# Seven block products in place of eight for five of 22 k-pairs of each down column pair

## The chip, the cores and the metric

The kernel runs on one core of one Trainium2 chip. The metric is device time in microseconds (us) of one execution; the kernel before has a median of 1750.02 us.

## The reference, cut to what matters

One decoder layer over 256 tokens of width 2048, in float32: an FFN, a mixing part (gated linear attention and dilated attention behind one input projection), an output projection, a second FFN. The change touches the two FFNs, above all their last product, `@ w_down`, with 5632 rows and 2048 columns.

```python
def swiglu(x, w_gate, w_up, w_down):
    return (jax.nn.silu(x @ w_gate) * (x @ w_up)) @ w_down
...
        x = x + FFN_RESIDUAL_WEIGHT * swiglu(rms_norm(x, ffn1_norm[l]), ffn1_w_gate[l], ffn1_w_up[l], ffn1_w_down[l])
        h = rms_norm(x, mix_norm[l])
        z = h @ w_in[l]
...
        x = x + FFN_RESIDUAL_WEIGHT * swiglu(rms_norm(x, ffn2_norm[l]), ffn2_w_gate[l], ffn2_w_up[l], ffn2_w_down[l])
    return x
```

## The kernel before

**Products.** Each float32 operand is split into a high and a low part (fp32r), and a product is three matmuls: high by high, high by low, low by high (`products`, lines 264, 266, 268). Activations stand transposed, 128 features by 256 tokens per k-tile: `hh` and `hl` (16 k-tiles) feed the gate, up and mixing products, `uh` and `ul` (44 k-tiles) the down products. The 256 tokens are two row blocks (t = 0, 1). A column pair is two blocks of 512 output columns and uses four PSUM banks. One k-tile of a column pair is a unit of 2 row blocks x 2 column blocks x 3 = 12 matmuls of 512 columns.

**Weights.** One DMA on SyncE's queue brings the weights of a k-pair (two k-tiles by 1024 columns, 1 MB) into one of three `raw` buffers. `prepare` splits a k-tile: ScalarE writes the high part `wh` (line 104), VectorE the low part `wl` (line 105), each 128 x 1024, into one of four buffers. `weights` keeps two prepared tiles ahead.

**Sevens.** In blocks 1 to 7 of the 11 gate-and-up blocks, k-pairs 2 and 5 (`GROUPS`) are multiplied as 2 x 2 blocks with seven products in place of eight (`seven_products`, lines 288 to 290): 21 matmuls in place of 24. These need sums of weights (`seven`, lines 228 and 236: a first and a last `raw` tile and two sums, so 3.5 splits in place of 2), sums of activations (`seven_forms`, lines 310 to 315, once per FFN, kept in `fh` and `fl`), four more banks for the products that go to more than one output, and five instructions that fold those banks into sums for the evacuation (lines 349 to 353). The four gate banks and the four of the sevens change places from block to block.

**Down.** `column_pair` runs the 44 units of each of the two column pairs in the order of k. At its end `evac` adds half of the result to the residual stream `xs` (line 454). In the first FFN each finished 128 x 512 block of `xs` is then normalised and transposed for the mixing part: for columns 0 to 1023 by `norm_moved` (VectorE transposes 32 x 32 squares, line 119; 16 small DMAs on GpSimd's queue, line 124, move them into `hh[8..15]`; `finish`, line 144 and `split`, writes `hh` and `hl` 0 to 7), for the rest by `norm_block` (TensorE, line 100).

**Order of the work.** Work beside the products stands in the list `later`; `column_pair` and `seven_pair` take from it at a steady rate, two steps a unit, over `span` steps. That is the order of the program's text. The order in which each engine issues is fixed when the program is built (`schedule_with_timeline_sim=True`), by a planner that has its own costs for every instruction and takes what it expects to be ready. Small 128 x 512 scratch tiles (`t512`: `sg`, `u`, `us`, `hf`) share four buffers.

Of the kernel before, what the change touches and what calls it, by code (L numbers as in the profile page):

```python
# [30 lines left out]
GROUPS = (2, 5)  # L31
SEVEN = range(1, 8)
TAIL = FT - 4 * SEVEN[-1] - 4
# [3 lines left out]
C_QG, C_KG, C_VG, C_GL, C_RG, C_QA, C_KA, C_VA = 0, 512, 1024, 2048, 2064, 3088, 4112, 5136  # L37


def layer_kernel(tc, x, xT, gains, gla_gate_up, gla_gate_bias, gla_out_norm, att_q_norm, att_k_norm,  # L40
# [6 lines left out]
    with ExitStack() as es:  # L47
# [27 lines left out]
        xs = cst.tile([P, NT, D], F32, name="xs")  # L75
        hh = cst.tile([P, KT, S], F32R, name="hh")
        hl = cst.tile([P, KT, S], F32R, name="hl")
# [7 lines left out]
        junk = cst.tile([P, 512], F32, name="junk")  # L85

# [46 lines left out]
        def norm_moved(t, c, gi):  # L133
# [13 lines left out]
            later.extend([lambda: None] * 4 + [finish])  # L147
# [13 lines left out]
        def ff_jobs(w):  # L161

            n = KT // 2
            for i in range(w.shape[0]):
                if i // n in SEVEN and i % n in GROUPS:
                    yield from ((w, i, part) for part in ("plain", "last", "sums", "more"))
                else:
                    yield from ((w, i, k) for k in range(2))

        jobs = [*ff_jobs(w_ff1)] + [(w_dn1, i, k) for i in range(w_dn1.shape[0]) for k in range(2)]  # L170
# [3 lines left out]
        jobs += [*ff_jobs(w_ff2)] + [(w_dn2, i, k) for i in range(w_dn2.shape[0]) for k in range(2)]  # L174
# [9 lines left out]
        def prepare():  # L184
# [15 lines left out]
            if k in ("last", "sums", "more"):  # L200
                return seven(k)
# [7 lines left out]
            if k == "plain":  # L209
                return seven(k)  # L210
# [9 lines left out]
        room = {}  # L220

        def seven(part):

            raw = raws[0].bitcast(F32)
            if part == "plain":
# [44 lines left out]
        later = []  # L270

# [4 lines left out]
        def seven_products(cs, ms, kp, first, last):  # L276
# [6 lines left out]
            fh, fl = room["fh"], room["fl"]  # L283
            a11, a12, a22 = [(hh[:, 2 * kp + k, tok[t]], hl[:, 2 * kp + k, tok[t]]) for t, k in ((0, 0), (0, 1), (1, 1))]
            s1, s3, s2, sa = [(fh[kp][:, i, :], fl[kp][:, i, :]) for i in range(4)]
# [17 lines left out]
        def seven_forms(kp):  # L303

            raw = room["rest"][0], room["rest"][1]
            full = raw[0].rearrange("p (k t q) -> p k t q", k=2, t=NT)
            sums = raw[1].rearrange("p (i q) -> p i q", i=4)
            ks = slice(2 * kp, 2 * kp + 2)
            nc.vector.tensor_add(raw[0].rearrange("p (k s) -> p k s", k=2), hh[:, ks, :].bitcast(F32), hl[:, ks, :].bitcast(F32))
            a11, a12, a21, a22 = full[:, 0, 0, :], full[:, 1, 0, :], full[:, 0, 1, :], full[:, 1, 1, :]  # L310
# [6 lines left out]
        def seven_pair(b, evac):  # L317

            cs = four_banks(b % 2)
            ms = None  # L320
            folds = []
            order[0] = 4 * (1 - b % 2)
            units = []
            for kp in range(KT // 2):
                units += [kp] if kp in GROUPS else [(2 * kp,), (2 * kp + 1,)]
            total = done = 0
            steps = 2 * (len(units) - len(GROUPS))
            step = 0
            for n, unit in enumerate(units):
                if isinstance(unit, tuple):  # L330
                    ws = [weights()]
                    for t in range(NT):
                        step += 1
                        total = max(total, done + len(later))
                        go = min(max(-(-total * step // steps) - done, 0), len(later))
# [4 lines left out]
                        products([cs[2 * t], cs[2 * t + 1]], t, [hacts[unit[0]]], ws, n == 0, n == len(units) - 1)  # L340
                    continue
                if ms is None:
                    ms = four_banks(1 - b % 2)
                last = unit == GROUPS[-1]
                seven_products(cs, ms, unit, unit == GROUPS[0], last)
                if last:
                    nat = [m.rearrange("p (a b) -> p b a", b=2) for m in ms]
                    p1, u, u2, u3 = [halves(a) for a in room["rest"]]
                    folds = [lambda: nc.scalar.activation(p1, nat[0], AF.Copy),
                             lambda: nc.vector.tensor_add(u, p1, nat[2]),  # L350
                             lambda: nc.vector.tensor_add(u2, u, nat[3]),
                             lambda: nc.vector.tensor_add(u, u, nat[1]),
                             lambda: nc.vector.tensor_add(u3, u2, nat[1])]
            for t in range(NT):
                rest = ((u, p1), (u3, u2))[t]
                evac(t, [c.rearrange("p (a b) -> p b a", b=2) for c in cs[2 * t:2 * t + 2]], rest)
# [516 lines left out]
```

## Time and profile before

| what | value |
|---|---|
| median of 3 runs | 1750.02 us (1748.29 to 1750.72) |
| profiled execution, its own time | 1748.53 us |
| its span, first to last instruction | 1746.8 us |
| granted TensorE clock over the span | 1.000 of full speed |
| weights read, queue of SyncE | 350.25 MB, 55.9% of 16 DMA engines |

The span is what the instructions cover; the profiled execution's own time is 1.7 us more. All terms below are read from this one execution. PE is TensorE's matmul, PEld its weight load, DVE VectorE, ACT ScalarE, POOL GpSimd, SP SyncE.

### The profile page before, as it was taken

How to read it: one execution, taken by the hardware profiler on the slowest of the kernel's cores; microseconds unless marked ns; L12 is line 12 of the kernel's file. 1: busy time of each engine (PE TensorE's matmuls, PEld its weight loads, DVE VectorE, ACT ScalarE, POOL GpSimd, SP SyncE). 2: the span in 40 equal slices, each digit the busy share in tenths (PEclk: the TensorE clock that was granted, in tenths of full speed). 3: DMA queues.
4: the chain of work that ended last, by engine and by line, in shares of the span. 5: the costliest groups of instructions: out<-in, count | busy, mean ns of one | idle time of the engine just before them, and what ended most of it. 6: DMA issues, size and time to landing. Idle time of an engine off the chain costs nothing.

```text
span 1746.8 us, 21964 instructions
## 1 busy us (share of the span) xinstructions
PE 1736.6 (99%) x8160; PEld 1515.7 (87%) x8160; DVE 1179.1 (68%) x1329; ACT 885.2 (51%) x1088; POOL 438.4 (25%) x870
## 2 busy tenths in 40 slices
PE   9999999999999999999999999999999999999999
PEld 7888888888888888888888888888888888888887
DVE  7888888855544656566655657788888955554544
ACT  7555555544444445565654545555555544444442
POOL 0333344443300421011000034333333444310000
PEclk9999999999999999999999999999999999999999
DMA  8666565766655666556444464666665666665653
GB/s 341 225 220 217 207 228 207 253 213 218 216 201 209 211 222 212 194 193 215 156 166 169 146 220 165 229 218 235 231 222 215 223 215 215 222 214 201 225 208 121
DMA packets 80843, 367.59 MB, mean 210 GB/s; under 512 B 19248, under 2 KB 36656, under 8 KB 38496
## 3 DMA queue, kind: packets, MB, share of 16 engines
q1 hardware_dynamic: 50864, 350.25, 55.9%
q0 software_dynamic: 29152, 14.87, 3.3%
q8 instruction: 64, 1.05, 0.2%
q10 hardware_dynamic: 720, 1.07, 0.2%
q14 instruction: 43, 0.35, 0.1%
HBM read 350.38 MB, written 2.10 MB: 202 GB/s over the span
## 4 chain that ended last, share of the span: by engine, by line
PE 90%; DMA 4%; DVE 4%; issue 1%; ACT 1%; POOL 1%; DVEq 0%; SPq 0%; ACTq 0%; POOLq 0%
PE acc L266 25%; PE acc L268 25%; PE acc L264 25%; PE tp L264 2%; PE tp L266 2%; PE tp L268 2%; DMA raw<-in_w_ff_dram 2%; DVE wl L105 2%; PE acc L290 1%; PE acc L289 1%; PE acc L288 1%; DMA hh<-us 1%; DMA ur<-us 1%; PE tp L100 1%; ACT wh L104 1%
## 5 line engine op out<-in xcount | busy, mean ns | idle before, releaser
L105 DVE TENSOR_TENSOR wl<-raw,wh 128x1024 fp32r<-128x1024 f32 (+1 forms) x658 | 796.3, 1219 | 456.9 <-ACT wh L104 454.6
L104 ACT ACTIVATE wh<-raw 128x1024 fp32r<-128x1024 f32 (+1 forms) x660 | 684.8, 1049 | 656.4 <-PE acc L268 535.8
L124 POOL DMA_DIRECT2D ur<-us x704 | 344.3, 497 | 551.5 <-issue 273.8
L266 PE MATMUL acc<-wl,hh 128*128 128x512 f32 x1376 | 416.8, 381 | 0.1
L268 PE MATMUL acc<-wh,hl 128*128 128x512 f32 x1376 | 414.9, 381 | 0.0
L264 PE MATMUL acc<-wh,hh 128*128 128x512 f32 x1376 | 409.1, 381 | 2.0 <-ACT wh L104 2.0
L264 PEld LDWEIGHTS acc<-wh,hh 128*128 128x128 f32 x1376 | 259.7, 189 | 39.3 <-ACT wh L104 2.7
L266 PEld LDWEIGHTS acc<-wl,hh 128*128 128x128 f32 x1376 | 259.6, 189 | 37.7 <-issue 1.0
L268 PEld LDWEIGHTS acc<-wh,hl 128*128 128x128 f32 x1376 | 259.8, 189 | 36.4 <-DVE hl L473 0.2
L266 PE MATMUL acc<-wl,uh 128*128 128x512 f32 x704 | 212.2, 379 | 0.0
L268 PE MATMUL acc<-wh,ul 128*128 128x512 f32 x704 | 212.0, 379 | 0.0
L264 PE MATMUL acc<-wh,uh 128*128 128x512 f32 x704 | 210.2, 379 | 0.0
L268 PEld LDWEIGHTS acc<-wh,ul 128*128 128x128 f32 x704 | 133.2, 189 | 18.9
L266 PEld LDWEIGHTS acc<-wl,uh 128*128 128x128 f32 x704 | 133.2, 189 | 18.8
L264 PEld LDWEIGHTS acc<-wh,uh 128*128 128x128 f32 x704 | 133.2, 189 | 18.7
L124 POOL DMA_DIRECT2D hh<-us x128 | 62.1, 500 | 175.2 <-issue 137.5
L153 POOL TENSOR_TENSOR rs<-a,mhalf 128x4 f32<-128x4 f32 (+1 forms) x12 | 17.4, 1454 | 257.9 <-DVE a L549 257.9
L264 PE MATMUL tp<-wh,hh 128*128 128x512 f32 x192 | 58.5, 379 | 0.0
L266 PE MATMUL tp<-wl,hh 128*128 128x512 f32 x192 | 57.1, 379 | 0.0
L268 PE MATMUL tp<-wh,hl 128*128 128x512 f32 x192 | 57.1, 379 | 0.0
L104 ACT ACTIVATE wh<-t 128x1024 fp32r<-128x1024 f32 x28 | 29.6, 1056 | 40.4 <-DVE t L228 30.0
L228 DVE TENSOR_TENSOR t<-raw 128x1024 f32<-128x1024 f32 x28 | 33.8, 1207 | 23.6 <-DMA raw<-in_w_ff_dram 23.6
(217 smaller groups left out, 1373.3 us busy)
## 6 DMA issues: line engine op xcount, KB each, us to landing
raw<-in_w_ff_dram SPq DMA_DIRECT2D x175, 1024.0 KB, 5.0
raw<-in_w_dn_dram SPq DMA_DIRECT2D x88, 1024.0 KB, 4.8
raw<-in_w_mix_dram SPq DMA_DIRECT2D x48, 1024.0 KB, 4.7
raw<-in_w_out_dram SPq DMA_DIRECT2D x16, 1024.0 KB, 4.8
ur<-us POOLq DMA_DIRECT2D x704, 16.0 KB, 3.7
xs<-in_x_dram SPq DMA_DIRECT2D x2, 1024.0 KB, 9.5
hh<-us POOLq DMA_DIRECT2D x128, 16.0 KB, 3.7
xt<-in_xT_dram SPq DMA_DIRECT2D x7, 256.0 KB, 6.4
```

The lines of the kernel that those rows point to most:

```text
L100: nc.tensor.transpose(dst, src, ident[:n, :n])
L104: nc.scalar.activation(dst_h, src, AF.Copy)
L105: nc.vector.tensor_sub(dst_l, src, dst_h.bitcast(F32))
L124: nc.gpsimd.dma_start(dst[32 * q:32 * q + 32, r * P:(r + 1) * P], src[32 * r:32 * r + 32, q * P:(q + 1) * P])
L153: nc.gpsimd.tensor_tensor(dst, src, mhalf[:, :src.shape[-1]], op=ALU.pow)
L228: nc.vector.tensor_add(room["sum"], b1, mid)
L264: nc.tensor.matmul(ps[j], lhsT=sh, rhs=alt(wh[:, j, :]), start=first and i == 0, stop=False)
L266: nc.tensor.matmul(ps[j], lhsT=sh, rhs=alt(wl[:, j, :]), start=False, stop=False)
L268: nc.tensor.matmul(ps[j], lhsT=sl, rhs=alt(wh[:, j, :]), start=False, stop=last and i == len(ws) - 1)
L288: nc.tensor.matmul(bank, lhsT=a[0], rhs=alt(ws[0][:, j, :]), start=start, stop=False)
L289: nc.tensor.matmul(bank, lhsT=a[0], rhs=alt(ws[1][:, j, :]), start=False, stop=False)
L290: nc.tensor.matmul(bank, lhsT=a[1], rhs=alt(ws[0][:, j, :]), start=False, stop=stop)
```

## The change

In each down column pair five of the 22 k-pairs become sevens. `DOWN_ORDERS` gives the order (g is a seven, s a plain k-pair); the sevens take k-pairs 0 to 4, the plain ones 5 to 21. The gate blocks keep their pattern `ssgssgss`, with k-pairs 0 and 1 as the sevens. `seven_forms` makes five sets of activation sums per FFN, at the start of its down stage, from `uh` and `ul` through two `t512` tiles; they lie in `hh[0..7]`, `hl[0..7]` and `hl[12..15]`, which nothing else needs then, the odd weight tile in `hl[8..11]`, and the weight sums in `urs`, the former two `ur` buffers. After the last seven of a column pair nine instructions fold the four extra banks: one copy, four sums, and four additions straight into `xs`. Since the activation sums are in `hh` and `hl` until the last seven of the second column pair, `finish` of `norm_moved` is held back until then (`held`, `holding`), and handed out over 20 steps of the last 24.

```diff
+FF_ORDERS = [_order("ssgssgss" if b in FF_SEVEN else "ssssssss") for b in range(FF // 512)]
+DOWN_ORDERS = [_order("ssssssgssgssgssgssgsss"), _order("sgsssgssgsssgssgssssss")]
...
-            later.extend([lambda: None] * 4 + [finish])
+            if holding[0]:
+                held.append(finish)
+            else:
+                later.extend([lambda: None] * 4 + [finish])
...
+        def jobs_of(w, orders):
+            for cp, order in enumerate(orders):
+                for kp, seven in order:
+                    for part in ("plain", "last", "sums", "more") if seven else (0, 1):
+                        yield w, cp * len(order) + kp, part
...
+        def seven_forms(acts, forms, full, sums):
+
+            for k, (ah, al, i) in enumerate(acts):
+                nc.vector.tensor_add(full[:, k * S:(k + 1) * S], ah[:, i, :].bitcast(F32), al[:, i, :].bitcast(F32))
...
-            split(room["fh"][kp], room["fl"][kp], sums)
+            split(*forms, sums)
+        def seven_pair(acts, pairs, forms, odd, evac, fold, span=None, final=False):
...
+                seven_products(cs, ms, acts[2 * u:2 * u + 2], forms[u], start, n == lastseven)
+                if n == lastseven:
+                    folds = fold([m.rearrange("p (a b) -> p b a", b=2) for m in ms])
+                    if holding[0] == 1:
+                        later.extend(held)
+                        held.clear()
+                        holding[0] = total = done = step = 0
+                        steps = 2 * (len(units) - n) - 6
...
-                        ur = fp.tile([P, 512], F32, name="ur", tag="ur", bufs=2)
+                        ur = urs[:, t, :]
...
+                dacts = [part(k) for k in range(FT)]
...
+                rooms["down"] = {"sum": urs, "wh": lent(hl, 8, 0), "wl": lent(hl, 10, 0)}
+                dforms = {kp: [lent(hh, 2 * kp, 1), lent(hl, 2 * kp, 1)] for kp in range(4)}
+                dforms[4] = [lent(hl, 12, 1), lent(hl, 14, 1)]
+                for kp in range(5):
+                    later.insert(min(2 * kp + 1, len(later)), lambda kp=kp: seven_forms(dacts[2 * kp:2 * kp + 2], dforms[kp], t512("full"), t512("sums")))
...
-                    column_pair([part(k) for k in range(FT)], evac, span=28 + 32 * cp, final=final and cp == 1)
+                    def fold(m, cp=cp):
+                        a, b = [halves(urs[:, i, :]) for i in range(2)]
+                        c = [[halves(xs[:, t, i * 512:(i + 1) * 512]) for i in (2 * cp, 2 * cp + 1)] for t in range(NT)]
+
+                        def add(c, a, f):
+                            return lambda: nc.vector.scalar_tensor_tensor(c, a, f, c, op0=ALU.mult, op1=ALU.add)
+                        return [lambda: nc.scalar.activation(a, m[0], AF.Copy),
+                                lambda: nc.vector.tensor_add(b, a, m[2]), add(c[0][1], a, 0.5),
+                                lambda: nc.vector.tensor_add(a, b, m[3]), add(c[1][1], a, 0.5),
+                                lambda: nc.vector.tensor_add(b, b, m[1]), add(c[0][0], b, -0.5),
+                                lambda: nc.vector.tensor_add(a, a, m[1]), add(c[1][0], a, -0.5)]
+
+                    holding[0] = NT - cp
+                    seven_pair(dacts, DOWN_ORDERS[cp], dforms, cp, evac, fold, span=28 if cp else 20, final=final and cp == 1)
```

## Rows read from the trace of the kernel before

**Rows 1.** Page, busy time of each engine.

```profile
PE 1736.6 (99%) x8160; PEld 1515.7 (87%) x8160; DVE 1179.1 (68%) x1329; ACT 885.2 (51%) x1088; POOL 438.4 (25%) x870
```

**Rows 2.** Page, chain of work that ended last, by engine.

```profile
PE 90%; DMA 4%; DVE 4%; issue 1%; ACT 1%; POOL 1%; DVEq 0%; SPq 0%; ACTq 0%; POOLq 0%
```

**Rows 3.** Timeline of PE, first down product (start us, us, what).

```profile
466.71 0.59 PE L268 MATMUL acc<-wh,ul 128*128 128x512 f32 x2
...
479.66 0.60 PE L268 MATMUL acc<-wh,ul 128*128 128x512 f32 x2
```

**Rows 4.** Windows: stretch, length, busy us (count) of PE PEld DVE ACT POOL, clock, DMA.

```profile
200.00:240.00 40.00, 40.00 (x187) 34.76 (x186) 35.49 (x41) 21.81 (x26) 15.62 (x32) 1.00 0.62 224
...
400.00:440.00 40.00, 40.00 (x187) 35.06 (x186) 22.27 (x22) 19.10 (x20) 15.63 (x32) 1.00 0.61 213
...
456.80:571.00 114.20, 114.20 (x531) 100.10 (x530) 57.99 (x51) 48.73 (x50) 15.64 (x32) 1.00 0.58 208
571.00:685.00 114.00, 114.00 (x530) 99.93 (x529) 63.17 (x61) 51.23 (x57) 35.52 (x72) 1.00 0.66 219
```

**Rows 5.** Waits of PE's weight loads in sevens (us in total, times, longest).

```profile
PEld tp L288 <- ACT wh L104: 1.4, 3, 0.7
PEld acc L288 <- ACT wh L104: 1.4, 3, 0.6
```

**Rows 6.** Groups by line: what VectorE does for a seven (busy us, mean ns).

```profile
L105 DVE TENSOR_TENSOR wl<-raw,wh 128x1024 fp32r<-128x1024 f32 (+1 forms) x658 | 796.3, 1219 | 456.9 <-ACT wh L104 454.6
...
L105 DVE TENSOR_TENSOR wl<-t,wh 128x1024 fp32r<-128x1024 f32 x28 | 34.1, 1219 | 0.2 <-ACT wh L104 0.2
L228 DVE TENSOR_TENSOR t<-raw 128x1024 f32<-128x1024 f32 x28 | 33.8, 1207 | 23.6 <-DMA raw<-in_w_ff_dram 23.6
...
L236 DVE TENSOR_TENSOR raw<-t,raw 128x512 f32<-128x512 f32 x28 | 19.4, 692 | 0.9
L105 DVE TENSOR_TENSOR swl<-raw,swh 128x512 fp32r<-128x512 f32 x28 | 19.3, 689 | 20.9 <-ACT swh L104 20.9
```

**Rows 7.** Instructions by line: an activation sum (min/median/max ns, first and last start).

```profile
L311 DVE TENSOR_TENSOR t<-t x4: 286/288/291, 12.3 to 1090.9; 128x128 f32<-128x128 f32 x4
...
L105 DVE TENSOR_TENSOR fl<-t,fh x4: 684/688/695, 15.8 to 1095.1; 128x512 fp32r<-128x512 f32 x4
```

**Rows 8.** Groups by line: a VectorE op on 256 columns; a fold on 512.

```profile
L353 DVE TENSOR_TENSOR t<-t,acc 128x512 f32<-128x512 f32 x14 | 9.6, 683 | 0.0
...
L473 DVE SCALAR_TENSOR_TENSOR hl<-xt,gT,hh 128x256 fp32r<-128x256 f32 x16 | 6.9, 481 | 0.0
```

**Rows 9.** Timeline of VectorE, then GpSimd, from 458 us (start us, us, what).

```profile
458.07 1.23 DVE L105 TENSOR_TENSOR wl<-raw,wh 128x1024 fp32r<-128x1024 f32 x1
...
477.34 0.69 DVE L105 TENSOR_TENSOR ul<-ur,uh 128x512 fp32r<-128x512 f32 x1
...
458.65 4.89 POOL L124 DMA_DIRECT2D ur<-us  x10 [22.38 <-ACT sg L414]
465.16 4.40 POOL L124 DMA_DIRECT2D ur<-us  x9 [1.62 <-DMA ur<-us]
471.15 6.47 POOL L124 DMA_DIRECT2D ur<-us  x13 [1.59 <-DMA ur<-us]
```

**Rows 10.** Page, DMA issues (KB each, us to landing).

```profile
ur<-us POOLq DMA_DIRECT2D x704, 16.0 KB, 3.7
```

**Rows 11.** Timeline of VectorE where one column pair follows the other.

```profile
569.43 0.69 DVE L454 SCALAR_TENSOR_TENSOR xs<-acc,xs 128x512 f32<-128x512 f32 x1 [1.36 <-PE acc L268]
...
571.77 0.70 DVE L119 STREAM_TRANSPOSE us<-xs 128x512 f32<-128x512 f32 x1
...
574.18 1.18 DVE L105 TENSOR_TENSOR wl<-raw,wh 128x1024 fp32r<-128x1024 f32 x1
577.86 2.36 DVE L105 TENSOR_TENSOR wl<-raw,wh 128x1024 fp32r<-128x1024 f32 x2 [2.49 <-ACT wh L104]
```

**Rows 12.** Line 144 in the first FFN's down (first and last start).

```profile
L144 DVE TENSOR_TENSOR hf<-hh,gT x4: 683/683/686, 588.7 to 640.5; 128x512 f32<-128x512 f32 x4
```

More of the change, by code (lines that the diff above doesn't have):

```diff
@@ L158, in norm_finish @@
             rsqrt(rt[:, t:t + 1], ssum[:, t:t + 1])
[L161 to L170, printed above, removed]
+        def jobs_of(w, orders):
[3 more added lines that the diff above has]
+                        yield w, cp * len(order) + kp, part
+        jobs = [*jobs_of(w_ff1, FF_ORDERS), *jobs_of(w_dn1, DOWN_ORDERS)]
         jobs += [(w_mix, i, k) for i in range(3 * KT // 2) for k in range(2)] + ["low"]
@@ L218, in prepare, with seven @@
             ready.append((wh, wl))
-        room = {}
-        def seven(part):
+        rooms = {}
+        def seven(part, w):
             raw = raws[0].bitcast(F32)
+            room = rooms["gate" if w is w_ff1 or w is w_ff2 else "down"]
             if part == "plain":
@@ L301, in seven_products @@
             product(cs[3], a22, ws, 1, False, False)
[L303 to L310, printed above, removed]
+        def seven_forms(acts, forms, full, sums):
+            for k, (ah, al, i) in enumerate(acts):
+                nc.vector.tensor_add(full[:, k * S:(k + 1) * S], ah[:, i, :].bitcast(F32), al[:, i, :].bitcast(F32))
+            a11, a21, a12, a22 = [full[:, i * P:(i + 1) * P] for i in range(4)]
+            sums = sums.rearrange("p (i q) -> p i q", i=4)
             nc.vector.tensor_sub(sums[:, 0, :], a22, a21)
@@ L314, in seven_forms @@
             nc.vector.tensor_add(sums[:, 3, :], a12, sums[:, 2, :])
-            split(room["fh"][kp], room["fl"][kp], sums)
[L317 to L331, printed above, removed]
+            split(*forms, sums)
+        def seven_pair(acts, pairs, forms, odd, evac, fold, span=None, final=False):
+            cs, ms, folds = four_banks(odd), None, []
+            order[0] = 4 * (1 - odd)
+            units = [u for kp, seven in pairs for u in ([kp] if seven else [(2 * kp,), (2 * kp + 1,)])]
+            lastseven = max(n for n, u in enumerate(units) if not isinstance(u, tuple))
+            steps = span or 2 * sum(isinstance(u, tuple) for u in units)
+            total = done = step = n = 0
+            while n < len(units):
+                u = units[n]
+                if isinstance(u, tuple):
+                    g = WBUF if final and n == len(units) - WBUF else 1
+                    ws = [weights() for _ in range(g)]
+                    last = n + g == len(units)
                     for t in range(NT):
@@ L334, in seven_pair @@
                         total = max(total, done + len(later))
[L335 removed]
+                        go = min(max(-(-total * min(step, steps) // steps) - done, 0), len(later))
                         done += go
@@ L339, in seven_pair @@
                             folds.pop(0)()
-                        products([cs[2 * t], cs[2 * t + 1]], t, [hacts[unit[0]]], ws, n == 0, n == len(units) - 1)
-                    continue
[L342 to L356, printed above, removed]
+                        now = [acts[v[0]] for v in units[n:n + g]]
+                        products(cs[2 * t:2 * t + 2], t, now, ws, n == 0, last, ((0,), (1,)) if g > 1 else ((0, 1),))
+                        if last:
+                            evac(t, [c.rearrange("p (a b) -> p b a", b=2) for c in cs[2 * t:2 * t + 2]])
+                    n += g
+                    continue
+                start = ms is None
+                if start:
+                    ms = four_banks(1 - odd)
+                seven_products(cs, ms, acts[2 * u:2 * u + 2], forms[u], start, n == lastseven)
[6 more added lines that the diff above has]
+                        steps = 2 * (len(units) - n) - 6
+                n += 1
         def column_pair(acts, evac, span=28, due=None, extra=None, final=False):
```

73 lines of the change are left out of this document (43 added, 30 removed).

## The prediction

> **What bounds the kernel now.** I read the busy times first: PE is busy 99% of the span [rows 1], and the chain of waits that ended last lies on PE for 90% [rows 2]. Matmul records overlap, so a busy PE need not be a full one; the timeline settles it. In the first down product two PE rows lie exactly five units of 12 matmuls apart, 479.66 - 466.71 = 12.95 us [rows 3]. That is 0.216 us a matmul without a gap, although each record lasts longer than that. The windows then show where this holds. Both down column pairs load weights on PE at the same density (100.10 us in 114.20, 99.93 in 114.00) as a gate stretch without sevens (35.06 in 40), and a gate stretch with sevens has a little less (34.76) [rows 4]. Its VectorE is at 35.49 of 40 us, 89%, where the down pairs have 57.99 of 114.20 and 63.17 of 114.00, 51% and 55% [rows 4]. So TensorE sets the time, one matmul after another, the granted clock is 1.00 in all four stretches, and the down stage has the room on VectorE that sevens need. What a seven costs when VectorE is nearly full is read from the waits of the existing sevens, below.
>
> **What is removed.** A seven has 21 matmuls where a k-pair has 24. There are 5 sevens in each of 2 column pairs in each of 2 FFNs, 20 in all, so 60 matmuls go: 8160 become 8100. They are 128 x 128 by 512 like the rest, so they are worth 60 x 0.216 = 12.95 us [rows 3]. The same weights are read; 1 MB per k-pair now has to come in 21 x 0.216 = 4.53 us at a seven, 231 GB/s, against 208 to 224 GB/s moved at a DMA share of 0.58 to 0.66 in these stretches [rows 4], so there is room. The gate blocks only change which k-pairs are sevens: nothing.
>
> **What is added on VectorE.** A plain k-pair costs two low splits, 2 x 1.22 = 2.44 us. A seven costs three of them (3.66), the wide weight sum (1.21), two narrow ones (2 x 0.69) and the odd tile's split (0.69), 6.94 us [rows 6], so 4.5 us more. A set of activation sums is two additions of 256 columns (nearest row 0.48 each), four of 128 columns (0.29 each) and a split of 512 (0.69): 2.8 us [rows 7, 8]. A fold has eight VectorE instructions of 512 columns at 0.68, 5.5 us [rows 8]. First column pair: 58.0 + 5 x 4.5 + 5 x 2.8 + 5.5 = 100 us in 114.2 - 3.2 = 111, 90%. Second: 63.2 + 22.5 + 5.5 = 91 in 111, 82%. The first is thus as full as the gate blocks, the second less. ScalarE gets 1.5 high splits a seven, a copy a fold and half a split a set; at 48.73 of 114.20 us [rows 4] it has room. None of this lies on PE's path as long as weights stay ahead of it. If that cover goes, PE waits for the low parts.
>
> **What the added work costs PE.** Three places, each bounded from both sides.
>
> At the sevens: PE's weight loads waited for ScalarE's high parts at line 288 six times, 2.8 us in all, over the 28 sevens of the gate blocks [rows 5], 0.1 us a seven, with VectorE at 89%. The most that one waited is 0.7. So 20 sevens cost 0 to 14 us, and I take the mean of those rows, 20 x 0.1 = 2.0 us, since the load on VectorE is the same or less.
>
> At the start of down: five sets are handed out within 13 steps, some 7 units or 18 us. In those VectorE would have 14.0 (sets) + 7 x 1.22 (splits) + about 2.9 (evacuation of the last gate block, four instructions of about 0.7) = 25.4 us, 7.3 more than there is. Weights stand about two units, 5.2 us, ahead of PE, so PE would wait 2.1 us. But the planner moves such work: the sets of the gate, handed out in block 1, ran from 12.3 us on [rows 7], and VectorE has idle time in the last gate block, 22.27 of 40 us being used in that kind of block [rows 4]. Nothing excludes 0, and 2.1 is the other end. I take 0.5 for each FFN, nearer to nothing, by the row of the early sets: 1.0 us.
>
> Where the second column pair follows the first: its first seven comes after one plain k-pair, where the gate always has two. The evacuation and two transposes hold VectorE until 574.2 now [rows 11]. In that order, wide sum, split, odd tile, narrow sums and split would take 5.7 us more, to 579.9; PE, which starts that pair near 571.8, would want the last of them 5.2 + 2.1 us later, at 579.1. So 0 to 0.8 us; the VectorE there waits 2.49 us for ScalarE soon after [rows 11], which says that it has slack, so I take 0.2 each: 0.4 us.
>
> **What moves.** The four held `finish` calls ran from 588.7 to 640.5 [rows 12], long before the mixing part, which starts near 685. Now they come in steps 5 to 20 of the last 24. The fourth is handed out two units, 5.2 us, before the end, and its output is first read four units into the mixing part, so it has 15 us for an addition and a split (0.69 + 1.05 + 0.69). Their DMAs, 64 issues on GpSimd's queue, still go early in the second column pair, and nothing but GpSimd's own work stands behind them. The extra banks are free by then: fold instruction 9 is given out three steps before the second pair starts. I cost these at nothing. If the cover is gone, the first products of the mixing part wait.
>
> **The sum.** -12.95 + 2.0 + 1.0 + 0.4 = -9.55 us. The profiled execution took 1748.53, so its counterpart comes to 1739.0; the median of the runs is 1.5 us above it, and 1750.02 - 9.55 = 1740.5 is the forecast.
>
> **The rivals.**
>
> *Every seven waits.* If each new seven waited as the worst of the gate's, 20 x 0.7 = 14 us [rows 5] would eat the gain: 1750.0 - 12.95 + 14 = 1751, no change; at half of it, 1744 to 1745. For it: the first column pair is at 90% of VectorE, and three sevens there lie only two plain k-pairs apart. Against it: the gate has the same spacing and load and lost 0.1.
>
> *The sets of sums stand in front of the splits (slower).* `full` and `sums` take `t512` buffers, of which the last gate block's two `us` hold two while GpSimd sends them off. If VectorE's queue has a set behind such a buffer, all splits behind it wait. GpSimd's first 16 issues run from 458.65 to about 468.1, the landing takes 3.7 [rows 9, 10], so the buffer is free near 471.8; set and split (2.8 + 1.2) end at 475.8. The last split before was done at 459.3 [rows 9], good for four units, so PE runs out of work near 467.2. That is a gap of 8.6 us in each FFN: 1750.0 - 12.95 + 2.0 + 17.2 = 1756.3. The kernel is slower by over 0.2% once each gap is over 7.2 us. Against it: `finish` of that block waits for the same DMAs and comes second in the text, yet it ran at 477.34 with splits put in front of it [rows 9]; the planner doesn't queue work before what it expects to be free. And the sets need two of four buffers only.
>
> *The normalised blocks are late.* If the four held calls slip past the end of the second pair, each costs about 2.4 us, 9.6 less the 5.2 us of cover: 4.4 us once, 1745. Against it: VectorE has 18% left there.
>
> *A matmul taken out gives back less than its spacing.* If PE were held by weight loads, it would be 1515.7/8160 = 0.186 us each [rows 1], 11.1 us in place of 12.95, so 1742.4. The row of 60 matmuls in 12.95 us speaks against it [rows 3]. The Trainium skill, page "TensorE: Matmul & The Clock Gate", section "Back-to-back issue gap", gives about 131 ns a matmul for 512 columns in a sustained stream. By that the gain would be an estimated 7.9 us before waits, and the time 1745.5; this trace does not agree, it has 216 ns, and the measurement decides.
>
> That the products are not removed can't be: the count is in the program.
>
> **How the numbers follow.** About 0.2%, 3.5 us, is what a measurement of this kernel can tell from no change. Forecast, 1736.5 to 1743: 0.71. Sevens or the seam wait for some of the gain, 1743 to 1746.5: 0.11. Late blocks or a smaller gain, also 1742 to 1746.5: 0.05. Nearly all eaten, 1746.5 to 1753.5: 0.08. The sets block the queue, over 1753.5: 0.05. So faster 0.87, same 0.08, slower 0.05. The lower end, 1736.5, leaves waits of half a microsecond in all (-12.95 + 0.5 from 1750.0 is 1737.5) and the 1 us by which runs differ. The upper end goes through the partly eaten cases to 1746.0, so that some 0.14 is left out.
>
> **What would show it.** Right: 8100 matmuls; PE's loads at the density of 100.1 in 114.2 in both down pairs, each some 3.2 us shorter; waits at lines 288 to 290 of 5 us at most over 48 sevens; VectorE near 90% in the first down pair; the held `finish` within the last 31 us of the second. Wrong: one gap of PE over 5 us at the start of a down stage (the sets), waits of over 0.5 us at most of the new sevens, or a PE wait for `hh` or `hl` where the mixing part begins.

## The result, and the profile after

The changed kernel takes 1736.47 us (median of 4 runs, 1736.13 to 1741.79) beside 1749.79 for the kernel before; ratio 0.9932, 95% interval 0.9911 to 0.9952. It is faster by 4.0 us more than the forecast said, and lies right at the lower end of the range, 1736.5. The ratio, that of the means, stands for 11.9 us; the medians lie 13.3 us apart, and the interval, 8.4 to 15.6 us, holds both. Its profiled execution took 1736.26 us, 12.27 less than that of before.

Lines have moved: 104 and 105 are now 113 and 114 (high and low split), 124 is 133 (moves), 144 is 153 (`finish`), 228 and 236 are 238 and 246 (weight sums), 264 to 268 are 274 to 278 and 288 to 290 are 298 to 300 (products), 454 is 483 (evacuation). In kernels with a line added above them they are one more.

The page after, busy time of each engine (answers to [rows 1]): 60 matmuls fewer, 12.3 us of loads fewer, 120 us of VectorE more.

```profile
PE 1725.2 (99%) x8100; PEld 1503.4 (87%) x8100; DVE 1299.5 (75%) x1535; ACT 921.3 (53%) x1142; POOL 438.9 (25%) x870
```

The windows of the four down column pairs after, columns as in [rows 4], which they answer to:

```profile
457.30:568.00 110.70, 110.70 (x514) 96.95 (x513) 95.13 (x121) 59.74 (x66) 15.63 (x32) 1.00 0.60 214
568.00:679.40 111.40, 111.15 (x514) 96.79 (x513) 85.00 (x92) 57.95 (x68) 35.53 (x72) 1.00 0.66 224
1508.70:1619.00 110.30, 110.30 (x512) 96.58 (x512) 94.83 (x121) 59.32 (x64) 15.64 (x32) 1.00 0.60 213
1619.00:1730.00 111.00, 111.00 (x516) 97.15 (x514) 78.08 (x79) 51.16 (x51) 0.00 (x0) 1.00 0.54 193
```

PE's loads have the density of before (96.95 in 110.70 is 0.876, as 100.10 in 114.20), lower only in the second row, where PE is busy 0.25 us less than the stretch. VectorE is busy 86%, 76%, 86% and 70% of the four stretches.

Where the profiled times differ, by stage, is read from PE's timeline: a down stage runs from its first matmul on `uh` to the first matmul behind it (in the second FFN, to the start of its last one). The profiled executions differ by 12.27 us; the two down stages make 12.25 of it.

| stage | before, us | after, us | difference |
|---|---|---|---|
| first 20 matmuls (warm-up), first FFN's gate | 455.29 | 455.81 | +0.5 |
| first down stage | 227.92 | 222.14 | -5.78 |
| mixing part and output projection | 378.11 | 378.14 | 0.0 |
| second FFN's gate | 451.76 | 451.15 | -0.6 |
| second down stage | 227.70 | 221.23 | -6.47 |

Thirty matmuls of 0.216 us are 6.47 us. The second down stage gave back just that; the first gave back 0.69 less. The waits of PE's weight loads in the first down stage after (us in total, times, longest) are the only ones; over the second, from 1508.7 to 1730, the same view is empty.

```profile
PEld acc L274 <- ACT wh L113: 0.6, 1, 0.6
PEld acc L298 <- ACT wh L113: 0.3, 1, 0.3
```

Both belong to one place, the first seven of the second column pair; this place, where one column pair follows the other, is called the seam below. PE's timeline after:

```profile
576.21 0.38 PE L300 MATMUL acc<-wh,hl 128*128 128x512 f32 x1
576.50 0.48 PE L298 MATMUL acc<-wh,hh 128*128 128x512 f32 x1
576.83 0.38 PE L298 MATMUL tp<-wh,uh 128*128 128x512 f32 x1
577.45 0.70 PE L274 MATMUL acc<-wh,uh 128*128 128x512 f32 x2 [0.25 <-ACT wh L113]
```

Starts there lie 0.29, 0.33 and 0.62 us apart in place of 0.216. VectorE's timeline after, at that place (answers to [rows 11]), and behind it the row of ScalarE that PE waited for:

```profile
569.04 0.70 DVE L128 STREAM_TRANSPOSE us<-xs 128x512 f32<-128x512 f32 x1
...
571.43 0.70 DVE L128 STREAM_TRANSPOSE us<-xs 128x512 f32<-128x512 f32 x1
572.06 1.18 DVE L114 TENSOR_TENSOR wl<-urs,wh 128x1024 fp32r<-128x1024 f32 x1
573.16 1.29 DVE L128 STREAM_TRANSPOSE us<-xs 128x512 f32<-128x512 f32 x2
574.38 0.65 DVE L246 TENSOR_TENSOR raw<-raw 128x512 f32<-128x512 f32 x1
576.49 5.77 DVE L114 TENSOR_TENSOR wl<-raw,wh 128x1024 fp32r<-128x1024 f32 x5 [1.46 <-ACT wh L113]
...
575.40 4.93 ACT L113 ACTIVATE wh<-raw 128x1024 fp32r<-128x1024 f32 x5 [3.50 <-DVE raw L246]
```

All four transposes (line 128; the row of 573.16 has two) and the additions of the evacuation stand in front of the last narrow weight sum, at 574.38. ScalarE sits idle for 3.50 us until that sum is there and writes its high part from 575.40 on; PE wants that part at 576.4 and gets it at 576.5; the high part of the next tile, behind it on ScalarE, is late too (577.45).

VectorE's timeline at the start of the first down stage after (answers to [rows 9]):

```profile
461.14 0.72 DVE L316 TENSOR_TENSOR full<-uh,ul 128x256 f32<-128x256 f32 x2
...
463.76 1.23 DVE L114 TENSOR_TENSOR wl<-raw,wh 128x1024 fp32r<-128x1024 f32 x1
...
484.23 0.69 DVE L114 TENSOR_TENSOR hl<-sums,hl 128x512 fp32r<-128x512 f32 x1
484.83 0.68 DVE L114 TENSOR_TENSOR ul<-urs,uh 128x512 fp32r<-128x512 f32 x1
485.55 1.22 DVE L238 TENSOR_TENSOR urs<-raw 128x1024 f32<-128x1024 f32 x1
...
489.44 3.50 DVE L114 TENSOR_TENSOR wl<-raw,wh 128x1024 fp32r<-128x1024 f32 x3
```

The first set of activation sums starts at 461.14, while GpSimd still sends off the `us` tiles; weight splits stand between the sets; the fifth set's split comes at 484.23. The last `finish` of the gate, which still reads `urs`, runs at 484.83, and only then can the first weight sum go into `urs` (485.55), 2.9 us before PE comes to the first seven (457.3 + 12 x 2.59 = 488.4).

The held `finish` calls of the first FFN after (answers to [rows 12]), and the split that ends the last of them, 38 us before the mixing part starts at 679.43:

```profile
L153 DVE TENSOR_TENSOR hf<-hh,gT x4: 685/688/691, 589.9 to 639.3; 128x512 f32<-128x512 f32 x4
...
641.08 0.69 DVE L114 TENSOR_TENSOR hl<-hf,hh 128x512 fp32r<-128x512 f32 x1
```

### The profile page after: what moved, and what is told of

It reads as the page before. It is cut to its first block, busy times and chain, and to the rows that moved or that the text cites. A ratio compares the mean times of both kernels' runs of the same rounds, so it can differ in the third digit from the quotient of the medians.

```text
span 1734.5 us, 22127 instructions
## 1 busy us (share of the span) xinstructions
PE 1725.2 (99%) x8100; PEld 1503.4 (87%) x8100; DVE 1299.5 (75%) x1535; ACT 921.3 (53%) x1142; POOL 438.9 (25%) x870
## 4 chain that ended last, share of the span: by engine, by line
PE 82%; DVE 9%; DMA 5%; issue 2%; ACT 1%; POOL 1%; SPq 0%; DVEq 0%; ACTq 0%
PE acc L276 20%; PE acc L278 20%; PE acc L274 20%; DVE wl L114 4%; DMA raw<-in_w_ff_dram 4%; PE tp L278 3%; PE tp L276 3%; PE tp L274 3%; PE acc L300 2%; PE acc L299 2%; PE acc L298 2%; ACT wh L113 1%; DVE raw L246 1%; DMA urs<-us 1%; DVE t L238 1%
## 5 line engine op out<-in xcount | busy, mean ns | idle before, releaser
L133 POOL DMA_DIRECT2D urs<-us x704 | 344.3, 497 | 551.9 <-issue 287.6
L276 PE MATMUL acc<-wl,uh 128*128 128x512 f32 x408 | 122.8, 379 | 0.0
L278 PE MATMUL acc<-wh,ul 128*128 128x512 f32 x408 | 122.5, 379 | 0.0
L274 PE MATMUL acc<-wh,uh 128*128 128x512 f32 x408 | 119.6, 379 | 0.2 <-ACT wh L113 0.2
L274 PEld LDWEIGHTS acc<-wh,uh 128*128 128x128 f32 x408 | 77.0, 189 | 11.6 <-ACT wh L113 0.6
L278 PEld LDWEIGHTS acc<-wh,ul 128*128 128x128 f32 x408 | 77.1, 189 | 11.0
L276 PEld LDWEIGHTS acc<-wl,uh 128*128 128x128 f32 x408 | 77.1, 189 | 10.9
```

Source lines behind the costliest of these rows:

```text
L133: nc.gpsimd.dma_start(dst[32 * q:32 * q + 32, r * P:(r + 1) * P], src[32 * r:32 * r + 32, q * P:(q + 1) * P])
L274: nc.tensor.matmul(ps[j], lhsT=sh, rhs=alt(wh[:, j, :]), start=first and i == 0, stop=False)
L276: nc.tensor.matmul(ps[j], lhsT=sh, rhs=alt(wl[:, j, :]), start=False, stop=False)
L278: nc.tensor.matmul(ps[j], lhsT=sl, rhs=alt(wh[:, j, :]), start=False, stop=last and i == len(ws) - 1)
```

## The experiments

All are edits of the changed kernel. Stage times are read as above; ratios are to the kernel before, run beside each (its medians there are 1749.17 to 1750.47). The first down stage of kernels with the changed kernel's first order (after, e2, e6, e9, e10) took 222.14 to 222.66 us, that of kernels with e1's order (e1, e8, e12) 221.44 to 221.92: with the same order of sevens it differs by up to 0.5 us.

| run | median, us | ratio, 95% interval | first down, us | second down, us |
|---|---|---|---|---|
| before | 1749.79 | | 227.92 | 227.70 |
| after | 1736.47 | 0.9932 (0.9911 to 0.9952) | 222.14 | 221.23 |
| e5, gate part alone | 1747.96 | 0.9987 (0.9978 to 0.9997) | 227.92 | 227.70 |
| e7, three sevens | 1741.81 | 0.9952 (0.9936 to 0.9968) | 224.45 | 223.82 |
| e1, second pair later | 1736.76 | 0.9931 (0.9913 to 0.9948) | 221.70 | 221.23 |
| e2, transposes later | 1736.87 | 0.9929 (0.9913 to 0.9945) | 222.42 | 221.23 |
| e10, none at the seam | 1739.14 | 0.9937 (0.9923 to 0.9950) | 222.14 | 221.23 |
| e11, no first norms | 1733.77 | 0.9917 (0.9902 to 0.9932) | 221.45 | 221.23 |
| e3, five in a row | 1780.73 | 1.0175 (1.0160 to 1.0190) | 244.97 | 242.57 |
| e4, first seven early | 1763.02 | 1.0076 (1.0061 to 1.0091) | 235.39 | 235.17 |
| e6, seven in FFN 2 | 1744.70 | 0.9967 (0.9954 to 0.9979) | 222.66 | 230.73 |
| e9, early, `urs` free | 1736.74 | 0.9925 (0.9910 to 0.9941) | 222.14 | 222.19 |
| e8, seven after six | 1741.71 | 0.9958 (0.9945 to 0.9970) | 221.44 | 226.62 |
| e12, seven, `urs` free | 1738.59 | 0.9937 (0.9925 to 0.9949) | 221.92 | 223.54 |

**Where the gain is: e5 and e7.** e5 takes the sevens out of the down stages and leaves the gate's new choice of k-pairs.

```diff
-        jobs = [*jobs_of(w_ff1, FF_ORDERS), *jobs_of(w_dn1, DOWN_ORDERS)]
+        jobs = [*jobs_of(w_ff1, FF_ORDERS), *jobs_of(w_dn1, [[(k, False) for k in range(22)]] * 2)]
...
-                    seven_pair(dacts, DOWN_ORDERS[cp], dforms, cp, evac, fold, span=28 if cp else 20, final=final and cp == 1)
+                    column_pair(dacts, evac, span=28 + 32 * cp, final=final and cp == 1)
```

> No sevens in the down column pairs, which run as before the change; the gate blocks keep the new choice of k-pairs (0 and 1) for their sevens. Theory A (the gain is the 60 matmuls of the down stages): within 1 us of before, 1749.0 to 1750.5; down stages of 227.7 to 227.9 us. Rival B (choosing other k-pairs in the gate gives part of it): 1747 or less.

Its down stages are those of before to the hundredth, and its profiled execution took 1748.26 us, 0.3 less than that of before. Its median lies between what the two theories said, 2.5 us under that of before, with an interval that just leaves out no change. The trace shows no stage with such a gain, so what the rest is stays open (the last section has a candidate). By the stage times the gain is in the down stages.

```diff
-DOWN_ORDERS = [_order("ssssssgssgssgssgssgsss"), _order("sgsssgssgsssgssgssssss")]
+DOWN_ORDERS = [_order("ssssssgsssssgsssssgsss"), _order("sgssssssgssssssgssssss")]
...
-                for kp in range(5):
+                for kp in range(3):
```

> Three sevens in place of five in each down column pair, three sets of activation sums. Theory A (each seven gives back three matmuls of 0.216 us and costs nothing but the wait at the seam): 36 matmuls, 7.8 us, less 0.7: 1749.8 - 7.1 = 1742.7; 0.65 us lost for each seven that is taken away. Rival B (the fold, the held blocks and the sums have a fixed cost that five sevens pay as well as three): more than 1744.

Against before, the second down stage is 3.88 us shorter, 18 matmuls of 0.216, and the first 3.47, which is that less 0.4 at the seam. Theory A holds: a seven's worth is its three matmuls, whether there are three or five, and the fold and the sets cost nothing that shows.

**The wait at the seam: e1, e2, e10, e11.** e1 puts a second plain k-pair in front of the first seven of the second column pair.

```diff
-DOWN_ORDERS = [_order("ssssssgssgssgssgssgsss"), _order("sgsssgssgsssgssgssssss")]
+DOWN_ORDERS = [_order("ssssssgssgssgssgssgsss"), _order("ssgssgssgsssgssgssssss")]
```

> The first seven of the second column pair comes after two plain k-pairs in place of one; all else as in the changed kernel. Theory A (the only cost in the down stages is VectorE falling behind at the seam, where evacuation and transposes stand in front of the first seven's sums): the gap of PE of 0.7 us near 576 us is gone, the first FFN's down stage takes 221.5 us in place of 222.1, the time is 1736.47 - 0.7 = 1735.8. Rival B (a first seven after an evacuation always waits, as in the gate blocks, which have two plain k-pairs in front of it and still wait 0.2 to 0.6 us in some blocks): a gap of 0.2 us or more stays, now about 5 us later.

The gap near 576 is gone, and none stands 5 us later, where rival B had one. A new one of 0.26 us came near 646, so the stage won 0.44 us; the median, 1736.76, does not show it. Then the transposes, with one plain k-pair kept.

```diff
+                            later.extend([lambda: None] * (4 if cp == 0 else 0))
                             done(t, c, blk)
```

> The normalisation of the blocks that the first column pair ends is handed out four steps (two units, 5.2 us) later for each row block; the order of sevens is that of the changed kernel. Theory A (the transposes on VectorE are what makes the first seven's narrow sums late): the gap of 0.7 us near 576 us shrinks to under 0.2, time 1735.8. Rival B (one plain k-pair is too little cover whatever else VectorE does): a gap of 0.5 us or more stays, time 1736.5.

The gap stayed at 0.70 us. e10 calls `done` for the first pair's blocks only after that pair, behind eight empty steps.

```diff
-                            done(t, c, blk)
+                            if cp or final:
+                                done(t, c, blk)
+                            else:
+                                pend.append((t, c, blk))
...
+                    if not cp and not final:
+                        later.extend([lambda: None] * 8)
+                        for p in pend:
+                            done(*p)
```

> In the first FFN the normalisation of the blocks that the first column pair ends is handed out only after the first seven of the second pair (e2 moved only two of the four transposes). Theory A (the transposes are what made the first seven's last weight sum late): the gap of 0.7 us near 576 us is gone, as at the same place of the second FFN, which has no transposes: first down stage 221.5 us. Rival B (one plain k-pair is too little cover): 222.1 us.

Again 0.70. Neither is a test: in both traces VectorE's order at the seam is that of the changed kernel, with the four transposes in the same places. The planner takes what it expects to be ready, and the transposes are ready as soon as the block is evacuated, whatever the text says. So e11 leaves them out.

```diff
-            later.append(lambda: (norm_moved if c < 2 else norm_block)(t, c, gi))
+            if c >= 2 or gi == 2:
+                later.append(lambda: (norm_moved if c < 2 else norm_block)(t, c, gi))
```

> Leaves out the transposes, moves and writes that normalise columns 0 to 1023 after the first FFN (the mixing part then reads what the activation sums left in hh and hl). e2 and e10 handed the transposes out later, but the planner put them back to the same place, so neither took them away. Theory A (the four transposes, 2.6 us of VectorE in front of the first seven's last weight sum, make the gap at the seam): the gap of 0.7 us near 576 us is gone, first down stage 221.5 us, as in the second FFN. Rival B (one plain k-pair is too little cover, the second FFN is spared for another reason): 222.1 us.

With the transposes go their moves and the held `finish` calls, so the mixing part works on other numbers, and of e11 only the first down stage counts. It takes 221.45 us, without a gap. VectorE's timeline in e11 has the last narrow sum at 572.03, 2.4 us earlier than after, right behind the evacuation:

```profile
568.50 1.88 DVE L483 SCALAR_TENSOR_TENSOR xs<-acc,xs 128x512 f32<-128x512 f32 x3
...
572.03 0.68 DVE L246 TENSOR_TENSOR raw<-raw 128x512 f32<-128x512 f32 x1
```

So the transposes make the wait, and one plain k-pair is cover enough without them, as it is in the second FFN.

**How near the edge the sevens stand: e3.**

```diff
-DOWN_ORDERS = [_order("ssssssgssgssgssgssgsss"), _order("sgsssgssgsssgssgssssss")]
+DOWN_ORDERS = [_order("ssssssgggggsssssssssss"), _order("ssssssgggggsssssssssss")]
```

> The five sevens of each column pair follow each other without plain k-pairs between, after six plain ones, in both column pairs. A seven takes 6.94 us of VectorE and 4.53 us of PE, so five in a row bring VectorE 12 us behind; weights stand 5.2 us ahead. Theory A (sevens are free only while VectorE's lead lasts, so their spacing matters): PE waits 5 to 8 us in each of the four column pairs, 20 to 32 us in all, time 1756 to 1768, slower than the kernel before although it has the same 8100 matmuls. Rival B (the queue of prepared weights, or the planner, evens it out): under 1 us a column pair, 1736 to 1740.

With the same 8100 matmuls it is 44 us slower than the changed kernel: PE loses 23.5 and 21.3 us in the two down stages. That is theory A's direction, but some 11 us a column pair where it had 5 to 8, and 1780.73 us where it had 1768 at most. The waits of VectorE (first) and of ScalarE from 484 to 530 us in e3 show what the theory left out, beside VectorE's own load:

```profile
DVE hl L114 <- ACT hl L113: 6.1, 1, 6.1
```

```profile
ACT wh L113 <- DVE raw L246: 10.8, 4, 3.2
ACT hl L113 <- PE acc L300: 7.2, 2, 6.2
```

The odd weight tile has a single buffer (`hl` 8 to 11). ScalarE waits for PE to be done with that of the seven before, and VectorE stands idle 6.1 us for ScalarE, at the time when it should run ahead; later ScalarE waits for VectorE's narrow sums. With two or three plain k-pairs between sevens, as in the changed kernel, PE waits for neither. How the 45 us divide between these two and VectorE's load was not measured apart.

**Why the first six k-pairs are plain: e4, e6, e9.**

```diff
-DOWN_ORDERS = [_order("ssssssgssgssgssgssgsss"), _order("sgsssgssgsssgssgssssss")]
+DOWN_ORDERS = [_order("ssgssgssgssgssgsssssss"), _order("sgsssgssgsssgssgssssss")]
```

> In the first column pair the first seven comes after two plain k-pairs (10 us) in place of six, so the five sets of activation sums compete with the sevens. Theory A (the sets are hidden because six plain k-pairs stand in front, with VectorE half idle): 5 sets of 2.6 us and two sevens at 6.9 us fall into the first 25 us, VectorE is some 5 us over, and PE waits 1 to 5 us in each FFN, time 1738 to 1746. Rival B (the planner puts the later sets off): under 0.5 us, 1736 to 1737.

In this order the weight sums also overwrite, in `urs`, part of the last gate block's activations before the last `finish` reads them, so its time is that of another computation with the same instructions. It is 27 us slower than the changed kernel: PE loses 13.9 us in the second down stage (235.17 - 221.23) and about as much in the first, far over the 1 to 5 us that theory A had. Some 10 to 11 us of each is one stand of PE, and most of the rest the slow matmuls behind it (last section). Waits from 462 to 486 us in e4, and VectorE's timeline there:

```profile
PE acc L298 <- ACT wh L113: 10.2, 1, 10.2
...
ACT wh L113 <- DVE urs L238: 3.7, 1, 3.7
```

```profile
461.70 0.72 DVE L316 TENSOR_TENSOR full<-uh,ul 128x256 f32<-128x256 f32 x2
...
475.87 0.68 DVE L114 TENSOR_TENSOR ul<-urs,uh 128x512 fp32r<-128x512 f32 x1
478.06 1.23 DVE L238 TENSOR_TENSOR urs<-raw 128x1024 f32<-128x1024 f32 x1 [1.51 <-DMA urs<-us]
```

All five sets run from 461.70 on, with one weight split between them, then a `finish`, and the weight sum waits 1.51 us more for GpSimd's moves into `urs`. PE has stood for 8 us by then, and stands until 480.56. Two causes are possible: the sets, or `urs`. e6 met the same from another side: it has seven sevens a pair in the second FFN, and its first pair starts with four plain k-pairs.

```diff
+DOWN_ORDERS2 = [_order("ssssgssgssgsgsgsgsgsss"), _order("sgssgssgsgssgsgssgssss")]
...
+                if final:
+                    dforms.update({kp: [lent(hh, 4 * kp - 12, 1), lent(hh, 4 * kp - 10, 1)] for kp in (5, 6)})
-                for kp in range(5):
+                for kp in range(7 if final else 5):
```

> In the second FFN, where nothing else needs hh 8 to 15, seven k-pairs of each down column pair are sevens in place of five: four more sevens, 12 matmuls less, 2.6 us. VectorE in its first down column pair goes from 95 us to about 95 + 2 x 4.5 + 2 x 2.6 = 109 us in 108.4 us. Theory A (VectorE's room is the bound on the number of sevens): PE waits in that column pair by about what VectorE is over, 1 to 4 us, so little or nothing is won: 1735 to 1738. Rival B (VectorE can be filled to the end): 1736.5 - 2.6 = 1733.9.

It lost 8.2 us on the changed kernel, more than either theory had. All that its second down stage loses against the matmuls alone, 12.1 us, lies at its first seven and right behind it (22 to 38 us into the stage), 8.3 us of it in one stand; where sevens and plain k-pairs alternate later, PE does not wait, though the stand had given VectorE a lead by then. e9 takes e4's order in the second FFN alone, and lets the last gate block's activations land elsewhere.

```diff
+DOWN_ORDERS2 = [_order("ssgssgssgssgssgsssssss"), _order("sgsssgssgsssgssgssssss")]
...
+                        if final and b == 10:
+                            ur = hh[:, 8 + 2 * t:10 + 2 * t, :].rearrange("p k s -> p (k s)")
+                            move_squares(ur, us.bitcast(F32R))
+                            ur = ur.bitcast(F32)
+                        else:
+                            move_squares(ur, us)
```

> In the second FFN alone the first seven of the first column pair comes after two plain k-pairs, as in e4; but the last gate block's transposed activations land in hh 8 to 11, so that the weight sums find their buffer (urs) free. Theory U (in e4 and e6 PE waited for urs, which GpSimd's DMAs fill and the last finish reads): most of the 13.9 us of waits of that stage in e4 are gone, it takes 221 to 225 us. Rival S (PE waited for the five sets of activation sums, which VectorE takes in one go): 8 us or more of wait stay, 229 to 236 us.

The second down stage takes 222.19 us: of the 13.9 us lost in e4 0.96 are left, at the second seven. Theory U is shown. VectorE's timeline in e9:

```profile
1513.33 0.72 DVE L317 TENSOR_TENSOR full<-uh,ul 128x256 f32<-128x256 f32 x2
...
1518.53 1.22 DVE L115 TENSOR_TENSOR wl<-urs,wh 128x1024 fp32r<-128x1024 f32 x1
...
1534.37 0.68 DVE L115 TENSOR_TENSOR ul<-hh,uh 128x512 fp32r<-128x512 f32 x1
```

The low split of the weight sum (`wl<-urs`, 1518.53) now stands between the first sets, and `finish` (1534.37) comes late without hurting anyone. With `urs` free, the five sets and so early a seven cost 0.96 us at most; it was the wait for `urs` that cost the rest. What that wait needs can be read from GpSimd's row in the changed kernel:

```profile
472.92 5.37 POOL L133 DMA_DIRECT2D urs<-us  x11 [2.02 <-DMA urs<-us]
```

The last move into `urs` is sent off by 478.3 and, with the 3.6 us from issue to landing that the page of the profile gives, lands near 482, 25 us into the stage, about as long as five plain k-pairs take; the last `finish` comes behind it. Six plain k-pairs are enough there (no wait in after), two were not (e4), nor four with seven sets (e6); five sevens behind three to five were not run.

**Are more sevens better: e8, e12.** e8 is e6 with six plain k-pairs in front, then sevens and plain ones in turn (`ssssssgsgsgsgsgsgsgsss`), and e1's order in the first FFN.

```diff
-DOWN_ORDERS = [_order("ssssssgssgssgssgssgsss"), _order("sgsssgssgsssgssgssssss")]
+DOWN_ORDERS = [_order("ssssssgssgssgssgssgsss"), _order("ssgssgssgsssgssgssssss")]
+DOWN_ORDERS2 = [_order("ssssssgsgsgsgsgsgsgsss"), _order("ssgssgsgsgssgsgssgssss")]
...
-                for kp in range(5):
+                for kp in range(7 if final else 5):
```

> The second FFN has seven sevens in each down column pair as in e6, but its first column pair starts with six plain k-pairs in place of four, and then alternates seven and plain; the first FFN has the order of e1. Theory A' (formed after e6: PE waits only where a first seven stands less than six plain k-pairs behind the last gate block; VectorE may be filled nearly to the end): the second down stage takes 227.7 - 84 x 0.216/2 = 218.6 us, the first 221.5, the time is 3 us below the changed kernel, 1733.4. Rival (VectorE's total, about 109 of 109 us in that column pair, is the bound): the second down stage takes 221 us or more, nothing won.

e8 is five microseconds slower than the changed kernel. GpSimd's last row and VectorE's timeline in e8, where PE comes to the first seven at 1508.4 + 31.1 = 1539.5:

```profile
1527.61 1.97 POOL L134 DMA_DIRECT2D urs<-us  x4 [0.19 <-issue]
...
1542.97 0.68 DVE L115 TENSOR_TENSOR ul<-urs,uh 128x512 fp32r<-128x512 f32 x1
1543.69 1.22 DVE L239 TENSOR_TENSOR urs<-raw 128x1024 f32<-128x1024 f32 x1
```

The moves are sent off by 1529.6, yet the last `finish` runs 13 us later, behind the two sets more, and the weight sum behind it. So here it is not GpSimd that holds `urs`, but a `finish` late in VectorE's queue. All of the 8.0 us that the stage loses (226.62 - 218.64, the time of its matmuls alone) are there: a stand of 4.6 us and the slow matmuls behind it; none is in the alternating part. So A' was wrong in its number of plain k-pairs: the place of the last `finish` counts. The stage came out in the rival's range, but not by the rival's cause. e12 is e8 with `urs` free as in e9 (through `hh` 12 to 15).

```diff
+                        if final and b == 10:
+                            ur = hh[:, 12 + 2 * t:14 + 2 * t, :].rearrange("p k s -> p (k s)")
```

> e8 with the one thing changed that e9 pointed to: in the second FFN the last gate block's transposed activations land in hh 12 to 15, so that the weight sums find urs free. Theory U (the 8.0 us of waits in e8 are the first seven's wait for urs, and alternating sevens fill VectorE without loss): second down stage 218.6 to 219.6 us in place of 226.6, first 221.4, time 3 us below the changed kernel, 1733.5. Rival (the seven sets of activation sums themselves hold VectorE): 3 us or more of wait stay, 221.6 us or more in that stage.

The 8.0 us at the first seven are gone, as theory U said, but 4.9 others have come (223.54 - 218.64), so the stage takes 2.3 us more than with five sevens, and theory U's other half, that alternating sevens fill VectorE without loss, is wrong. Waits of PE's loads in its second down stage, the windows of its two column pairs, and the longest wait of the second pair:

```profile
PEld tp L300 <- DVE wl L115: 2.9, 4, 1.6
PEld acc L300 <- DVE wl L115: 1.5, 1, 1.5
```

```profile
1508.75:1619.00 110.25, 108.48 (x496) 92.93 (x495) 101.49 (x141) 59.77 (x68) 15.55 (x32) 1.00 0.57 203
1619.00:1732.00 113.00, 111.90 (x519) 97.88 (x518) 88.92 (x93) 54.85 (x57) 0.00 (x0) 1.00 0.54 198
```

```profile
1661.60 0.48 PE L300 MATMUL acc<-wl,hh 128*128 128x512 f32 x1 [1.10 <-DVE wl L115]
```

Now PE waits mostly for VectorE's low splits (`wl`). Some 3.5 us lie in the first pair, at its second, fourth, fifth and sixth seven, with VectorE at 92% of the stretch; some 1.4 lie in the second, where VectorE is at 79%, at a seven with a single plain k-pair in front of it. So with `urs` out of the way VectorE is the bound, and by these places it is the room between neighbouring sevens that counts and not only the share over a column pair; wider spacing with seven sevens was not run. No version here that computes the same beats the changed kernel by more than its runs can tell; e1 is 0.44 us better in the trace.

## Why the prediction was right in direction and too small

- **The matmuls.** 60 x 0.216 = 12.95 us: right, to 0.01 us in the second FFN, and again in e7. The Trainium skill's 131 ns (page "TensorE: Matmul & The Clock Gate", section "Back-to-back issue gap") would have made 3.9 us of the second down stage's 6.47; the trace has 216 ns.
- **The waits at the sevens, 2.0 us: the step that failed.** The term was mis-sized: no new seven waited but the one at the seam, which had a term of its own, so it measured 0. I spread the gate's 2.8 us [rows 5] over 28 sevens, but those are six waits in six blocks, each at the first seven behind a block's evacuation; that the evacuation makes them is read from the place alone. The profile after shows the same in the first FFN; waits of PE's loads from 165 to 310 us, at 183.7, 224.3, 264.7 and 305.1, one for each of four blocks with two sevens:

```profile
PEld tp L298 <- ACT wh L113: 1.1, 2, 0.6
PEld acc L298 <- ACT wh L113: 0.7, 2, 0.4
```

  In the down stages only the seam has a first seven so close behind an evacuation.
- **The seam, 0.4 us.** 0.69 in the first FFN, inside the 0 to 0.8 of the bound, and nothing in the second, whose evacuation has no transposes. That the transposes and the evacuation hold up the last narrow sum was right (e11), though what PE waited for was its high part, and not the low split at the end of the sum.
- **The sets at the start of down, 1.0 us.** It measured 0. "Handed out within 13 steps" was misread: the last gate block hands out its first `finish` already, so the list that the sets go into is shorter, and the last set is handed out in step 18 of 20; in the trace they spread over 24 us, 461.14 to 484.9.
- **VectorE.** 90% and 82% forecast, 86% and 76% measured: added durations count overlaps twice. Three splits in a row take 3.50 us (489.44), not 3 x 1.22, and the 121 instructions of the first pair last some 102 us taken singly, close to the 100 of the forecast, where VectorE is busy 95.13 us.
- **Held blocks.** No wait where the mixing part begins, as forecast. But the sign that they run within the last 31 us did not come: they ran from 589.9 on, as in before, so the planner had moved them forward, and the cover that was priced was not needed.
- **The rivals.** None came. The slower one was near in kind: a buffer that GpSimd's moves hold makes PE stand for 10.4 us in e4, but it is `urs` in front of the weight sums, not `us` in front of the sets.
- **The remainder.** -12.95 + 0.69 = -12.26 is the difference of the profiled executions (-12.27, the two gates' changes nearly cancelling). The medians differ by 13.3, 1 us more, and the means by 11.9; the last section has what runs differ by. Of the 4.0 us by which the forecast was short, the terms above explain 2.7 (12.26 - 9.55); the rest, 1.3, is within the interval, and no run shows a cause for it.

## What to carry to other kernels

Where TensorE runs without gaps, a matmul taken out is worth its spacing in the timeline, and what decides the rest is whether the engine that prepares operands keeps its lead at the few places where something else stands in its queue; look for waits by place, not by their mean. Before you lend a buffer to a new use, ask when its last reader of the old use runs; here that one date fixed how early the new work could start. And with a planner that orders by readiness, putting a call later in the text moves nothing unless a dependency does.

## What the runs showed of the hardware

Profiled executions with the same work in their first 20 us differ by some 2 us there. In eight of the fourteen (before, after, e1, e3, e5, e8, e11, e12) the granted clock of that stretch is 1.00, with 66 to 72 matmuls done; in six (e2, e4, e6, e7, e9, e10) it is 0.91, with 59 to 64. Window from 0 to 20 us, after, then e2:

```profile
0.00:20.00 20.00, 16.63 (x70) 13.91 (x71) 14.98 (x32) 13.97 (x23) 0.89 (x5) 1.00 0.89 323
```

```profile
0.00:20.00 20.00, 15.59 (x60) 12.44 (x61) 14.38 (x32) 13.13 (x23) 0.89 (x5) 0.91 0.91 323
```

Ten matmuls are 2.2 us, and e2's profiled run took 1738.99 us, its others 1735.95 to 1737.49. e10's down stages are those of the changed kernel to the hundredth, yet three of its four runs took 1739.0 to 1739.3, the profiled one, with 0.91, among them. In both cases PE starts and stops while the first weights arrive. The trace of before has no such dip, and with 1748.53 us it is one of the fastest runs of before; that some of the others had one, which could make the 1 us above and a part of e5's 2.5, was not seen.

A long wait costs more than itself. Windows of e4, then one of e8:

```profile
470.00:481.00 11.00, 0.76 (x3) 0.44 (x2) 8.55 (x20) 3.66 (x7) 6.89 (x15) 0.74 0.08 24
481.00:486.00 5.00, 4.75 (x13) 3.29 (x13) 4.89 (x5) 3.88 (x5) 0.00 (x0) 0.55 0.24 59
486.00:500.00 14.00, 14.00 (x66) 12.28 (x65) 11.20 (x11) 7.08 (x9) 0.00 (x0) 1.00 0.59 226
```

```profile
1546.00:1552.00 6.00, 5.65 (x12) 4.02 (x13) 5.95 (x6) 4.02 (x5) 0.00 (x0) 0.50 0.35 119
```

After PE stood from 470 to 480.5, the granted clock was 0.55 from 481 to 486, near the lower of its two levels (1.2 and 2.4 GHz), with 13 matmuls where 23 would fit, and 1.00 again from 486 on. In e8 PE stood from 1541.2 to 1546.1, and the clock was 0.50 from 1546 to 1552, with 12 matmuls where 28 would fit. A matmul there starts 0.43 us after the one before, in place of 0.216; this makes some 3 us of what each of the stages of e4, e6 and e8 lost.
